# A hybrid layer on one core: attention scores head by head, with stacked queries and doubled keys

## The chip, the core and the metric

The kernel runs on one core of one Trainium2 chip. The core has five engines with an instruction queue each: TensorE (PE; its weight loads are shown apart as PEld), VectorE (DVE), ScalarE (ACT), GpSimd (POOL) and SyncE (SP), which here only issues DMAs. Operands lie in the on-chip memory SBUF, with 128 partitions; TensorE writes its products to PSUM, which this kernel uses as eight banks of 128 x 512 fp32.

The metric is the time of one execution in device microseconds. The kernel before takes 480.91 us, the median of three runs (480.37 to 481.25).

## What is computed

One layer for one sequence of 512 tokens of width 1024. Cut to its core:

```python
xn   = rmsnorm(h, norm_gain)
proj = xn @ w_in                  # split into aq ak av ag bq bf bi bg gate_a gate_b
qa, ka = rmsnorm(heads(aq)), rmsnorm(heads(ak))      # 8 heads x 64
ya = moba_attention(qa, ka, heads(av), rel_bias)     # softmax(q k^T / 8 + bias[bucket(distance)]) v
ya = (ya * silu(ag)) @ w_up_a
yb = hgrn2_chunkwise(silu(bq), kb(bf), bi, log_f(bf))  # gated linear recurrence, 4 heads x 128
yb = (rmsnorm(yb) * silu(bg)) @ w_up_b
merged = sigmoid(gate_a) * ya + sigmoid(gate_b) * yb
h = h + merged @ w_out
h = h + (p @ w_ple) * sigmoid(h @ w_ple_gate)
```

The sequence has two blocks of 256 keys and up to three blocks may be chosen, so every query attends to all keys up to its own position: the attention is causal and dense, with a bias by distance.

## The kernel before

**Numbers in two parts.** Large products are made in three: a value x is held as hi + lo, where hi is x rounded to the type fp32r (written by ScalarE) and lo the rest (written by VectorE), and hi·hi, hi·lo and lo·hi are summed in PSUM (`split`, `scale_split`, `mm3`, L189 to L253). A column block of weights (128 x 1024 values, 512 KB) is loaded by SP into one of two raw buffers `wf`, split into `wh` and `wl` (three buffers each), and used for 24 products of 512 columns. `weight` (L238) splits two blocks ahead (`LD = 2`).

**Main sequence.** TensorE goes through: the token-major projections bi and av, the first recurrence head's bf and bq, then aq and ak (queries and keys), then the list `ORDER` (L48) of feature-major blocks bg, ag, bf, gb, ga, then eight ub blocks (up-projection of the recurrence), eight ua blocks (of the attention), eight h blocks (output) and eight g and pe blocks (gated per-layer embedding).

**Side work and its order.** TensorE's order is the order in which the Python program issues it; the other engines are scheduled by the framework, with a priority raised by `AHEAD` for some. The program keeps a clock `now` in microseconds. Each product of the main sequence adds its cost (`tick`) and then lets generators whose due time has come issue their instructions (`run_due`, L107). A generator that yields y is due again y us later; `cost` adds time without looking at the generators. Generators run for the normalisation, the recurrence (`hgrn_intra`, `hgrn_out`), the preparation of queries and keys (`qk_norm`) and `attention`. `drain(name)` (L764) advances the clock in half microseconds, with no product of the main sequence, until the named part is done; ub waits in this way for the recurrence, ua for the attention.

**Queries and keys** (`qk_norm`, L635). The four token blocks of a projection are copied, squared, summed by head and scaled. 14 us later, for each of four head pairs, four 128 x 128 transposes put the pair's features on partitions (head 2i on partitions 0 to 63, head 2i+1 on 64 to 127), and `scale_split` makes hi and lo tiles: `qh`, `ql`, `kh`, `kl`, four of each, 16 tiles of pool `A`.

**Attention** (`attention`, L666). The queries are taken in `STEPS` (L31): blocks 0 and 1 of 128 queries together, then block 2, then block 3; block qb sees 128·(qb+1) keys. There are 12 steps, one for each head pair and entry of `STEPS`. In a step `scores` (L671) issues, for each query block, three products for each of the two heads; head j uses partitions 64j to 64j+63 of both operands, so that the two heads' products lie in two halves of the array (the profile writes 64*128), and they write to two banks of tag `a`. The softmax then takes, for each head and query block: VectorE adds the bias and finds the extreme (L689), ScalarE takes the exponential with its sum (L691), VectorE inverts the sum (L692) and scales (L693). One step later `transposed` (L697) transposes the probabilities of both heads, 128 x 128 at a time, and ScalarE copies them to SBUF (`ptS`). When the three steps of a pair are through, `out_values` (L711) multiplies by the values (o), VectorE gates the result (`ya`, L724), and `split` makes `yah` and `yal`, which the ua blocks read. A step is spread over `AP` = 12.2 us of the planner's clock: 0.3 of it before the transposes, 0.25 between them and the scores, 0.45 behind the scores. The bias of a head (128 x 512) is read by a DMA from a row in DRAM (`ed`), into a pool `T` of three.

**Recurrence.** `hgrn_intra` issues its products in two groups (lpb, lpa); ahead of each, while attention runs, `beside_attention` (L436) waits until attention has gone a step further or `BESIDE` = 5 us have passed.

Of the kernel before, what the change touches and what calls it, by code (L numbers as in the profile page):

```python
# [21 lines left out]
NT = S // 128  # L22
# [8 lines left out]
STEPS = ((0, 1), (2,), (3,))  # L31

HP = 3.1
AP = 12.2
H0 = 8.0
XN = 3.0

RT = 8.0

BESIDE = 5.0  # L40

LD = 2

# [15 lines left out]
def hybrid_layer_kernel(  # L59
# [24 lines left out]
    ctx.enter_context(tc.manual_schedule(engines=ENG))  # L84


    BUFS = {"w": 2, "wh": 3, "wl": 3, "A": 16, "X": 16, "YB": 8, "H": 12, "T": 3, "Q": 4, "KT": 2, "P": 4, "PT": 2,
            "PT0": 2, "PT2": 2, "SG": 4, "YS": 1, "VV": 8, "s32": 1, "st": 1, "ps": 8}

    def unit(tag, name, dt=F32, shape=(128, 512)):  # L90
        return sb.tile(list(shape), dt, tag=tag, bufs=BUFS[tag], name=name)

    def bank(tag, name):
        return psum.tile([128, 512], F32, tag=tag, bufs={"mm": 4, "g": 2, "a": 2}[tag], name=name)
# [98 lines left out]
    def scale_split(hi, lo, src, g):  # L193
        A.activation(hi, src, AF.Copy, scale=g)
        V.scalar_tensor_tensor(lo, src, g, hi.bitcast(F32), op0=OP.mult, op1=OP.subtract)
# [235 lines left out]

    hg = {}

    runs = [1000]

    def beside_attention():  # L436
        seen, until = runs[0], now[0] + BESIDE
        if seen < 1000:
            yield lambda: runs[0] > seen or now[0] >= until

    def hgrn_gates(h, F, Q):
        a = unit("H", f"ha{h}")
        A.activation(a, F, AF.Abs)
# [20 lines left out]
    def hgrn_intra(h):  # L464
# [52 lines left out]
        yield HP  # L517
        k16 = kq(16)
        yield HP
        yield from beside_attention()  # L520
        lpa = bank("g", f"lpa{h}").rearrange("p (l c t) -> p l c t", l=4, c=NT)
        for c in range(NT):
            o, i = c * 128, 64 * (c % 2)
# [20 lines left out]
        for b in (8, 4, 2):  # L544
            ks.append(kq(b))
            yield HP
        yield from beside_attention()
        for i, k_ in enumerate(ks):
            diag(lpa[:, 1 + i], k_, k_, LEVELS[1 + i])

# [82 lines left out]


    def qk_norm(name, banks, g, res):  # L635
        hs = [unit("A", f"{name}h{i}", R) for i in range(HPAIRS)]
        ls = [unit("A", f"{name}l{i}", R) for i in range(HPAIRS)]
        raws = []
        ss = cst.tile([128, NT, HEADS], F32, name=name + "ss")
        y = cst.tile([128, NT, HEADS], F32, name=name + "y")  # L640
        t_ = cst.tile([128, NT, HEADS], F32, name=name + "t")
        for t in range(NT):
            raw = unit("P", f"{name}r{t}")
            A.activation(raw, banks[t], AF.Copy)
            sq = unit("PT", f"{name}q{t}")
            A.activation(sq, raw, AF.Square)
            V.tensor_reduce(ss[:, t], sq.rearrange("p (h d) -> p h d", h=HEADS), axis=AX.X, op=OP.add)
            raws.append(raw)
        V.tensor_scalar(ss, ss, 1.0 / 64, None, op0=OP.mult)
        rsqrt(y, t_, ss)  # L650
        for t in range(NT):
            r3 = raws[t].rearrange("p (h d) -> p h d", h=HEADS)
            V.tensor_tensor(r3, r3, y[:, t, :, None].to_broadcast([128, HEADS, 64]), op=OP.mult)
        yield 14.0
        for i in range(HPAIRS):
            tp = bank("a", f"{name}tp{i}")
            for t in range(NT):
                PE.transpose(tp[:, t * 128:t * 128 + 128], raws[t][:, i * 128:i * 128 + 128], ident)
            cost(0.44)
            with tc.high_priority(offset=AHEAD):  # L660
                scale_split(hs[i], ls[i], tp, g)
            res.append((hs[i], ls[i]))
            yield 1.3
        done.add(name)

    def attention(qn, kn, va, sags, res):  # L666
        def blocks(qbs):

            return [(qb, sum(128 * (b + 1) for b in qbs[:i]), 128 * (qb + 1)) for i, qb in enumerate(qbs)]

        def scores(hp, qbs, T):  # L671
            (qh, ql), (kh, kl) = qn[hp], kn[hp]
            prs = []

            sps = [bank("a", f"s{hp}{qbs[0]}{j}") for j in range(2)]
            for qb, o, nk in blocks(qbs):
                qs = slice(qb * 128, qb * 128 + 128)
                for i, (a, b) in enumerate(((qh, kh), (ql, kh), (qh, kl))):
                    for j in range(2):
                        js = slice(64 * j, 64 * j + 64)  # L680
                        PE.matmul(sps[j][:, o:o + nk], a[js, qs], b[js, :nk], start=(i == 0), stop=(i == 2))  # L681
                cost(3 * max(0.107, nk * 0.00042))
            with tc.high_priority(offset=AHEAD):
                for j in range(2):
                    pr = unit("P", f"p{hp}{qbs[0]}{j}")
                    for qb, o, nk in blocks(qbs):
                        p_ = pr[:, o:o + nk]
                        st = unit("ps", f"ps{hp}{qb}{j}", shape=(128, 4))
                        V.tensor_tensor_reduce(p_, sps[j][:, o:o + nk], T[j][:, nk - 1::-1], -1.0, 3e38,  # L689
                                               OP.add, OP.min, st[:, 0:1])  # L690
                        A.activation(p_, p_, AF.Exp, bias=st[:, 0:1], scale=-1.0, accum_out=st[:, 1:2])  # L691
                        V.reciprocal(st[:, 2:3], st[:, 1:2])  # L692
                        V.tensor_scalar(p_, p_, st[:, 2:3], None, op0=OP.mult)  # L693
                    prs.append(pr)
            return prs

        def transposed(hp, qbs, prs):  # L697
            n = sum(qb + 1 for qb in qbs)
            pts = []
            for j in range(2):  # L700
                tp = bank("a", f"pt{hp}{qbs[0]}{j}")
                for kb in range(n):
                    PE.transpose(tp[:, kb * 128:kb * 128 + 128], prs[j][:, kb * 128:kb * 128 + 128], ident)  # L703
                cost(0.11 * n)
                pt = unit("PT" if n == NT else f"PT{qbs[0]}", f"ptS{hp}{qbs[0]}{j}", shape=(128, n * 128))
                with tc.high_priority(offset=AHEAD):
                    A.activation(pt, tp[:, :n * 128], AF.Copy)  # L707
                pts.append(pt)
            return pts

        def out_values(hp, pts):  # L711

            o = bank("mm", f"o{hp}")
            for qbs, pt in zip(STEPS, pts):
                for qb, o0, nk in blocks(qbs):
                    qs = slice(qb * 128, qb * 128 + 128)
                    for kb in range(qb + 1):
                        for j in range(2):
                            h0 = hp * 128 + 64 * j
                            PE.matmul(o[64 * j:64 * j + 64, qs], va[kb][:, h0:h0 + 64],  # L720
                                      pt[j][:, o0 + kb * 128:o0 + kb * 128 + 128], start=(kb == 0), stop=(kb == qb))
            cost(1.5)
            ya = unit("YS", f"ya{hp}")
            V.tensor_tensor(ya, o, sags[hp], op=OP.mult)  # L724
            h_ = unit("A", f"yah{hp}", R)
            l_ = unit("A", f"yal{hp}", R)
            split(h_, l_, ya)
            res.append((h_, l_))
            done.add(f"ya{hp}")

        while not {"q", "k"} <= done:
            yield lambda: {"q", "k"} <= done
        yield 3.0
        runs[0] = 0
        NS = len(STEPS)
        steps = [(hp, i) for hp in range(HPAIRS) for i in range(NS)]
        T, prs, pts = {}, {}, {}
        for n in range(len(steps) + 1):
            if n >= 2:
                yield AP * 0.3  # L740
            if 1 <= n <= len(steps):
                hp, i = steps[n - 1]
                pts[n - 1] = transposed(hp, STEPS[i], prs.pop(n - 1))
                yield AP * 0.25
            if n < len(steps):
                hp, i = steps[n]
                if i == 0:
                    for j in range(2):
                        t = unit("T", f"bias{hp}{j}")
                        row = ed[2 * hp + j:2 * hp + j + 1, :]  # L750
                        nc.sync.dma_start(t, bass.AP(tensor=row.tensor, offset=row.offset,
                                                     ap=[[1, 128], [1, 512]]))
                        T[hp, j] = t
                prs[n] = scores(hp, STEPS[i], [T[hp, 0], T[hp, 1]])
            if n >= 1 and steps[n - 1][1] == NS - 1:
                hp = steps[n - 1][0]
                while f"ag{hp}" not in done:
                    yield lambda: f"ag{hp}" in done
                out_values(hp, [pts.pop(n - NS + i) for i in range(NS)])
            runs[0] += 1  # L760
            yield AP * 0.45
        runs[0] += 1000

    def drain(name):  # L764

# [233 lines left out]
```

## Time and profile before

| what | before |
|---|---|
| median of three runs | 480.91 us |
| span of the profiled execution | 479.0 us |
| mean granted TensorE clock | 0.995 |
| first and last score product (start) | 140.1, 321.1 us |
| first and last transpose of probabilities | 149.4, 332.5 us |
| last product with values (start) | 338.3 us |
| first ub, first ua block | 329.7, 355.0 us |
| DMA traffic | 48.41 MB |

The profile shows one execution. Its table of engines gives busy time, share of the span and number of instructions. A row of a timeline gives the start, the duration, engine, line, operation, output and inputs, the shape (for a product: rows * columns of the array and the moving operand), how many are merged, and, in brackets, how long the engine was idle before it and what ended the idle time. Durations of products overlap their successors, so a product's price is the distance from start to start. A row of a list of waits names who waited for whom: total us, times, the longest. A row of the windows gives, behind the stretch and its length, the busy time of PE, PEld, DVE, ACT and POOL with the number of instructions, the granted TensorE clock, the DMA share and GB/s. A row of DMA issues gives tensors, queue, count, size and the median time to landing.

### The profile page before, as it was taken

How to read it: one execution, taken by the hardware profiler on the slowest of the kernel's cores; microseconds unless marked ns; L12 is line 12 of the kernel's file. 1: busy time of each engine (PE TensorE's matmuls, PEld its weight loads, DVE VectorE, ACT ScalarE, POOL GpSimd, SP SyncE). 2: the span in 40 equal slices, each digit the busy share in tenths (PEclk: the TensorE clock that was granted, in tenths of full speed). 3: DMA queues.
4: the chain of work that ended last, by engine and by line, in shares of the span. 5: the costliest groups of instructions: out<-in, count | busy, mean ns of one | idle time of the engine just before them, and what ended most of it. 6: DMA issues, size and time to landing. Idle time of an engine off the chain costs nothing.

```text
span 479.0 us, 7949 instructions
## 1 busy us (share of the span) xinstructions
PE 471.2 (98%) x3162; PEld 386.4 (81%) x3162; DVE 300.6 (63%) x601; ACT 269.4 (56%) x476; POOL 14.4 (3%) x30
## 2 busy tenths in 40 slices
PE   9999999999997999999999999999999999999996
PEld 7788888788875878878888788878888888888886
DVE  4769683957795784696757946435458854543332
ACT  5757665547695786687757766656324532243211
POOL 0014000000000001000010000000000000000000
PEclk9999999999998999999999999999999999999999
DMA  7542222332221222124212322124333544323211
GB/s 225 196 151 103 89 88 89 116 129 88 89 87 47 89 89 90 48 85 133 90 46 76 98 93 83 29 90 131 77 100 115 207 146 148 98 96 115 90 44 44
DMA packets 17941, 48.41 MB, mean 101 GB/s; under 512 B 2248, under 2 KB 2888, under 8 KB 17904
## 3 DMA queue, kind: packets, MB, share of 16 engines
q1 hardware_dynamic: 17616, 47.82, 30.8%
q8 instruction: 24, 0.39, 0.4%
q0 software_dynamic: 144, 0.09, 0.1%
q14 instruction: 13, 0.11, 0.1%
q10 hardware_dynamic: 144, 0.01, 0.0%
HBM read 45.79 MB, written 2.12 MB: 100 GB/s over the span
## 4 chain that ended last, share of the span: by engine, by line
PE 67%; ACT 1%; DVE 0%; issue 0%; DVEq 0%
PE gb L251 9%; PE g L251 9%; PE h L251 9%; PE ga L251 9%; PE ub L251 5%; PE ua L251 5%; PE ag L251 3%; PE bq L251 2%; PE bg L251 2%; PE bf L251 2%; PE pe L251 2%; PE o L720 2%; PE s L681 2%; PE pt L703 2%; PE lpa L501 1%; PE hds L581 0%
## 5 line engine op out<-in xcount | busy, mean ns | idle before, releaser
L190 ACT ACTIVATE wh<-wf 128x1024 fp32r<-128x1024 f32 (+1 forms) x81 | 77.6, 958 | 121.6 <-PE g L251 20.4
L191 DVE TENSOR_TENSOR wl<-wf,wh 128x1024 fp32r<-128x1024 f32 (+1 forms) x81 | 90.0, 1112 | 67.6 <-ACT wh L190 65.8
L251 PE MATMUL g<-hh,wh 128*128 128x512 f32 (+1 forms) x72 | 26.3, 365 | 0.0
L251 PE MATMUL g<-hl,wh 128*128 128x512 f32 (+1 forms) x72 | 26.3, 365 | 0.0
L251 PE MATMUL g<-hh,wl 128*128 128x512 f32 (+1 forms) x72 | 26.3, 365 | 0.0
L251 PE MATMUL ga<-xh,wh 128*128 128x512 f32 x64 | 26.0, 406 | 0.0
L251 PE MATMUL gb<-xh,wh 128*128 128x512 f32 x64 | 25.5, 398 | 0.0
L251 PE MATMUL ga<-xh,wl 128*128 128x512 f32 x64 | 25.0, 391 | 0.0
L251 PE MATMUL gb<-xh,wl 128*128 128x512 f32 x64 | 25.0, 390 | 0.0
L251 PE MATMUL gb<-xl,wh 128*128 128x512 f32 x64 | 25.0, 390 | 0.0
L251 PE MATMUL ga<-xl,wh 128*128 128x512 f32 x64 | 24.9, 390 | 0.0
L251 PE MATMUL h<-mh,wh 128*128 128x512 f32 x64 | 24.9, 389 | 0.0
L251 PE MATMUL h<-ml,wh 128*128 128x512 f32 x64 | 24.9, 389 | 0.0
L251 PE MATMUL h<-mh,wl 128*128 128x512 f32 x64 | 24.9, 389 | 0.0
L691 ACT ACTIVATE p<-p,ps 128x128 f32<-128x128 f32 (+3 forms) x32 | 17.6, 550 | 8.7 <-DVE ps L689 8.6
L689 DVE CUSTOM_DVE_ANT_0 p<-s,bias 128x128 f32<-128x128 f32 (+3 forms) x32 | 14.1, 486 | 7.5 <-PE s L681 7.5
L889 DVE TENSOR_TENSOR hf<-h,xres 128x512 f32<-128x512 f32 x8 | 5.5, 692 | 18.2 <-PE h L251 18.2
L707 ACT ACTIVATE ptS<-pt 128x384 f32<-128x384 f32 (+1 forms) x24 | 11.5, 524 | 7.5 <-PE pt L703 7.5
L251 PEld LDWEIGHTS g<-hh,wl 128*128 128x128 f32 x72 | 13.6, 189 | 2.2
L251 PEld LDWEIGHTS g<-hl,wh 128*128 128x128 f32 x72 | 13.6, 189 | 2.2
L480 ACT ACTIVATE hx<-hx 128x512 f32<-128x512 f32 x24 | 14.6, 627 | 1.2 <-DVE hx L479 0.9
L251 PEld LDWEIGHTS g<-hh,wh 128*128 128x128 f32 x72 | 13.6, 189 | 2.1
(326 smaller groups left out, 1245.8 us busy)
## 6 DMA issues: line engine op xcount, KB each, us to landing
wf<-in_w_tr_dram SPq DMA_DIRECT2D x32, 512.0 KB, 3.4
wf<-in_w_tok_dram SPq DMA_DIRECT2D x15, 512.0 KB, 3.4
wf<-in_w_up_dram SPq DMA_DIRECT2D x16, 256.0 KB, 2.6
wf<-in_w_o_dram SPq DMA_DIRECT2D x8, 512.0 KB, 3.3
wf<-in_w_g_dram SPq DMA_DIRECT2D x8, 512.0 KB, 3.5
bias<-ed SPq DMA_DIRECT2D x8, 256.0 KB, 3.4
xres<-in_xT_dram SPq DMA_DIRECT2D x8, 256.0 KB, 2.9
xr<-in_xT_dram SPq DMA_DIRECT2D x7, 256.0 KB, 5.8
```

Of the source, the lines that this page charges most:

```text
L190: A.activation(hi, src, AF.Copy)
L191: V.tensor_tensor(lo, src, hi.bitcast(F32), op=OP.subtract)
L251: PE.matmul(ps, a[:, k, :], b[k], start=(n == 0), stop=(n == tot - 1))
L480: A.activation(x, x, AF.Exp)
L501: PE.matmul(d, l[:, o:o + 32], m, start=True, stop=True)
L681: PE.matmul(sps[j][:, o:o + nk], a[js, qs], b[js, :nk], start=(i == 0), stop=(i == 2))
L689: V.tensor_tensor_reduce(p_, sps[j][:, o:o + nk], T[j][:, nk - 1::-1], -1.0, 3e38, OP.add, OP.min, st[:, 0:1])
L691: A.activation(p_, p_, AF.Exp, bias=st[:, 0:1], scale=-1.0, accum_out=st[:, 1:2])
L703: PE.transpose(tp[:, kb * 128:kb * 128 + 128], prs[j][:, kb * 128:kb * 128 + 128], ident)
L707: A.activation(pt, tp[:, :n * 128], AF.Copy)
L720: PE.matmul(o[64 * j:64 * j + 64, qs], va[kb][:, h0:h0 + 64], pt[j][:, o0 + kb * 128:o0 + kb * 128 + 128], start=(kb == 0), stop=(kb == qb))
L889: V.tensor_tensor(t, ps, xres, op=OP.add)
```

## The change

**Operands.** `qk_norm` ends in one of two new generators. `stacked_queries` makes one tile `qs` per head with 128 rows: the head's own 64 partitions hold hi, the other 64 hold lo of the same head (ScalarE writes the own half, VectorE the other). `doubled_keys` makes `kh` and `kl` for each head: the own half is written by ScalarE and VectorE, and two DMAs on SP's queue copy each half to the other 64 partitions, 16 DMAs of 128 KB in all. Queries and keys fill 24 tiles of pool `A` in place of 16; the pool grows from 16 to 24, and the DMA scratch in the compiler's call is set to 1024.

**Scores.** For each head and query block two products over all 128 rows are summed: [hi; lo] of the query with [kh; kh], then with [kl; kl]. This also adds lo·lo, which the kernel before left out.

**Order.** Attention goes through 24 steps (8 heads x 3) with `AP` = 6.1 in place of 12; the transposes of a step come `LAG` = 2 steps behind its scores in place of one; `out_values` comes at the start of the step behind the last transposes of a pair. The first two biases are loaded ahead of the steps, each further one two heads ahead. `beside_attention` goes; 2.5 us are yielded in its place, whether attention runs or not.

```diff
-AP = 12.2
+AP = 6.1
+LAG = 2
...
-BESIDE = 5.0
...
-    BUFS = {"w": 2, "wh": 3, "wl": 3, "A": 16, ...
+    BUFS = {"w": 2, "wh": 3, "wl": 3, "A": 24, ...
...
-        yield from beside_attention()
+        yield 2.5
...
+    def stacked_queries(raws, g, res):
+        for i in range(HPAIRS):
+            tp = bank("a", f"qtp{i}")
+            for t in range(NT):
+                PE.transpose(tp[:, t * 128:t * 128 + 128], raws[t][:, i * 128:i * 128 + 128], ident)
+            cost(0.44)
+            with tc.high_priority(offset=AHEAD):
+                for j in range(2):
+                    qs = unit("A", f"qs{2 * i + j}", R)
+                    own, other = slice(64 * j, 64 * j + 64), slice(64 - 64 * j, 128 - 64 * j)
+                    A.activation(qs[own], tp[own], AF.Copy, scale=g[own])
+                    V.scalar_tensor_tensor(qs[other], tp[own], g[own], qs[own].bitcast(F32),
+                                           op0=OP.mult, op1=OP.subtract)
+                    res.append(qs)
+            yield 1.5
+
+    def doubled_keys(raws, g, res):
...
+            for j in range(2):
+                kh = unit("A", f"kh{2 * i + j}", R)
+                kl = unit("A", f"kl{2 * i + j}", R)
+                own, other = slice(64 * j, 64 * j + 64), slice(64 - 64 * j, 128 - 64 * j)
+                with tc.high_priority(offset=AHEAD):
+                    scale_split(kh[own], kl[own], tp[own], g[own])
+                for k_ in (kh, kl):
+                    nc.sync.dma_start(k_[other].bitcast(F32), k_[own].bitcast(F32))
+                res.append((kh, kl))
+            yield 1.5
...
-                for i, (a, b) in enumerate(((qh, kh), (ql, kh), (qh, kl))):
-                    for j in range(2):
-                        js = slice(64 * j, 64 * j + 64)
-                        PE.matmul(sps[j][:, o:o + nk], a[js, qs], b[js, :nk], start=(i == 0), stop=(i == 2))
-                cost(3 * max(0.107, nk * 0.00042))
+                for i, k_ in enumerate(kn[h]):
+                    PE.matmul(sp[:, o:o + nk], qn[h][:, qs], k_[:, :nk], start=(i == 0), stop=(i == 1))
+                cost(2 * (nk + 32) / 2400)
...
-            cost(1.5)
+            cost(2.5)
...
+        T = {0: bias(0), 1: bias(1)}
         yield 3.0
...
+        steps = [(h, i) for h in range(HEADS) for i in range(NS)]
+        prs, pts = {}, {}
+        pending = None
+        for n in range(len(steps) + LAG + 1):
+            if pending is not None:
+                while f"ag{pending}" not in done:
+                    yield lambda: f"ag{pending}" in done
+                out_values(pending, pts)
+                pending = None
+            if LAG <= n < len(steps) + LAG:
+                h, i = steps[n - LAG]
+                pts[h, i] = transposed(h, STEPS[i], prs.pop(n - LAG))
+                if i == NS - 1 and h % 2:
+                    pending = h // 2
+                yield AP * 0.4
+            if n < len(steps):
+                h, i = steps[n]
+                prs[n] = scores(h, STEPS[i], T[h])
+                if i == 1 and h + 2 < HEADS:
+                    T[h + 2] = bias(h + 2)
+            yield AP * (0.6 if n >= LAG else 0.8)
...
-    nc = _bacc.Bacc("TRN2", target_bir_lowering=False, num_devices=1)
+    nc = _bacc.Bacc("TRN2", target_bir_lowering=False, num_devices=1,
+                    dynamic_dma_scratch_size=1024)
```

More of the change, by code (lines that the diff above doesn't have):

```diff
@@ L84, in hybrid_layer_kernel @@
     ctx.enter_context(tc.manual_schedule(engines=ENG))
-    BUFS = {"w": 2, "wh": 3, "wl": 3, "A": 16, "X": 16, "YB": 8, "H": 12, "T": 3, "Q": 4, "KT": 2, "P": 4, "PT": 2,
+    BUFS = {"w": 2, "wh": 3, "wl": 3, "A": 24, "X": 16, "YB": 8, "H": 12, "T": 3, "Q": 4, "KT": 2, "P": 4, "PT": 2,
             "PT0": 2, "PT2": 2, "SG": 4, "YS": 1, "VV": 8, "s32": 1, "st": 1, "ps": 8}
@@ L432, in hybrid_layer_kernel @@
     hg = {}
[L434 to L439, printed above, removed]
     def hgrn_gates(h, F, Q):
@@ L546, in hgrn_intra @@
             yield HP
-        yield from beside_attention()
+        yield 2.5
         for i, k_ in enumerate(ks):
@@ L635, in qk_norm @@
     def qk_norm(name, banks, g, res):
-        hs = [unit("A", f"{name}h{i}", R) for i in range(HPAIRS)]
-        ls = [unit("A", f"{name}l{i}", R) for i in range(HPAIRS)]
         raws = []
@@ L654, in qk_norm @@
         yield 14.0
+        if name == "q":
+            yield from stacked_queries(raws, g, res)
+        else:
+            yield from doubled_keys(raws, g, res)
+        done.add(name)
+    def stacked_queries(raws, g, res):
         for i in range(HPAIRS):
-            tp = bank("a", f"{name}tp{i}")
+            tp = bank("a", f"qtp{i}")
             for t in range(NT):
@@ L660, in qk_norm @@
             with tc.high_priority(offset=AHEAD):
[L661 to L664, printed above, removed]
+                for j in range(2):
[8 more added lines that the diff above has]
+        for i in range(HPAIRS):
+            tp = bank("a", f"ktp{i}")
+            for t in range(NT):
[11 more added lines that the diff above has]
+            yield 1.5
     def attention(qn, kn, va, sags, res):
@@ L669, in blocks, with scores @@
             return [(qb, sum(128 * (b + 1) for b in qbs[:i]), 128 * (qb + 1)) for i, qb in enumerate(qbs)]
[L671 to L675, printed above, removed]
+        def scores(h, qbs, T):
+            sp = bank("a", f"s{h}{qbs[0]}")
             for qb, o, nk in blocks(qbs):
                 qs = slice(qb * 128, qb * 128 + 128)
-                for i, (a, b) in enumerate(((qh, kh), (ql, kh), (qh, kl))):
-                    for j in range(2):
-                        js = slice(64 * j, 64 * j + 64)
-                        PE.matmul(sps[j][:, o:o + nk], a[js, qs], b[js, :nk], start=(i == 0), stop=(i == 2))
-                cost(3 * max(0.107, nk * 0.00042))
-            with tc.high_priority(offset=AHEAD):
[L684 to L695, printed above, removed]
@@ L697, in transposed @@
-        def transposed(hp, qbs, prs):
-            n = sum(qb + 1 for qb in qbs)
[L699 to L709, printed above, removed]
+                for i, k_ in enumerate(kn[h]):
+                    PE.matmul(sp[:, o:o + nk], qn[h][:, qs], k_[:, :nk], start=(i == 0), stop=(i == 1))
@@ new lines, in scores @@
+                cost(2 * (nk + 32) / 2400)
+            with tc.high_priority(offset=AHEAD):
+                pr = unit("P", f"p{h}{qbs[0]}")
+                for qb, o, nk in blocks(qbs):
+                    p_ = pr[:, o:o + nk]
+                    st = unit("ps", f"ps{h}{qb}", shape=(128, 4))
+                    V.tensor_tensor_reduce(p_, sp[:, o:o + nk], T[:, nk - 1::-1], -1.0, 3e38,
+                                           OP.add, OP.min, st[:, 0:1])
+                    A.activation(p_, p_, AF.Exp, bias=st[:, 0:1], scale=-1.0, accum_out=st[:, 1:2])
+                    V.reciprocal(st[:, 2:3], st[:, 1:2])
+                    V.tensor_scalar(p_, p_, st[:, 2:3], None, op0=OP.mult)
@@ new lines, in scores, with transposed @@
+            return pr
+        def transposed(h, qbs, pr):
+            n = sum(qb + 1 for qb in qbs)
+            tp = bank("a", f"pt{h}{qbs[0]}")
+            for kb in range(n):
+                PE.transpose(tp[:, kb * 128:kb * 128 + 128], pr[:, kb * 128:kb * 128 + 128], ident)
+            cost(0.11 * n)
+            pt = unit("PT" if n == NT else f"PT{qbs[0]}", f"ptS{h}{qbs[0]}", shape=(128, n * 128))
+            with tc.high_priority(offset=AHEAD):
+                A.activation(pt, tp[:, :n * 128], AF.Copy)
+            return pt
@@ L711, in out_values @@
         def out_values(hp, pts):
             o = bank("mm", f"o{hp}")
-            for qbs, pt in zip(STEPS, pts):
+            for i, qbs in enumerate(STEPS):
                 for qb, o0, nk in blocks(qbs):
@@ L720, in out_values @@
                             PE.matmul(o[64 * j:64 * j + 64, qs], va[kb][:, h0:h0 + 64],
-                                      pt[j][:, o0 + kb * 128:o0 + kb * 128 + 128], start=(kb == 0), stop=(kb == qb))
-            cost(1.5)
+                                      pts[2 * hp + j, i][:, o0 + kb * 128:o0 + kb * 128 + 128],
+                                      start=(kb == 0), stop=(kb == qb))
+            cost(2.5)
             ya = unit("YS", f"ya{hp}")
@@ L729, in out_values, with bias @@
             done.add(f"ya{hp}")
+        def bias(h):
+            t = unit("T", f"bias{h}")
+            row = ed[h:h + 1, :]
+            nc.sync.dma_start(t, bass.AP(tensor=row.tensor, offset=row.offset, ap=[[1, 128], [1, 512]]))
+            return t
         while not {"q", "k"} <= done:
             yield lambda: {"q", "k"} <= done
+        T = {0: bias(0), 1: bias(1)}
         yield 3.0
-        runs[0] = 0
         NS = len(STEPS)
-        steps = [(hp, i) for hp in range(HPAIRS) for i in range(NS)]
@@ L737, in attention @@
[L737 to L744, printed above, removed]
-            if n < len(steps):
[L746 to L761, printed above, removed]
@@ L762, in attention @@
-        runs[0] += 1000
+        steps = [(h, i) for h in range(HEADS) for i in range(NS)]
[13 more added lines that the diff above has]
+                yield AP * 0.4
+            if n < len(steps):
+                h, i = steps[n]
[3 more added lines that the diff above has]
+            yield AP * (0.6 if n >= LAG else 0.8)
```

## The prediction, made before the changed kernel ran

> **What bounds the kernel now.** I read the table of engines first, then what TensorE waits for.
>
> ```profile
> PE 471.2 (98%) x3162; PEld 386.4 (81%) x3162; DVE 300.6 (63%) x601; ACT 269.4 (56%) x476; POOL 14.4 (3%) x30
> ```
>
> ```profile
> PE pt L703 <- DVE p L693: 2.4, 2, 1.9
> ```
>
> TensorE is busy for 471.2 of 479.0 us, so the time is the length of TensorE's instruction stream, plus the few places where it stops. The only wait of weight in that list is 2.4 us, where the first transposes of probabilities wait for VectorE's scaling. Everything on the other engines is free as long as it does not make TensorE wait. The timeline of TensorE shows what the wait really costs:
>
> ```profile
> 147.06 0.39 PE L251 MATMUL ag<-xh,wl 128*128 128x512 f32 x1
> 149.37 0.90 PE L703 MATMUL pt<-ident,p 128*128 128x128 f32 x4 [1.92 <-DVE p L693]
> 150.75 0.69 PE L703 MATMUL pt<-ident,p 128*128 128x128 f32 x2 [0.48 <-DVE p L693]
> 151.09 0.78 PE L251 MATMUL ag<-xh,wh 128*128 128x512 f32 x1
> 151.66 0.63 PE L251 MATMUL ag<-xl,wh 128*128 128x512 f32 x1
> ...
> 153.37 0.40 PE L251 MATMUL ag<-xh,wl 128*128 128x512 f32 x1
> 153.61 0.40 PE L251 MATMUL ag<-xh,wh 128*128 128x512 f32 x1
> ```
>
> ```profile
> 150.00:160.00 10.00, 9.52 (x40) 7.23 (x39) 4.46 (x12) 5.08 (x10) 0.00 (x0) 0.83 0.34 104
> ```
>
> The projections start every 0.227 us elsewhere, and here, after the pause, every 0.43 us for five products; the granted clock of these ten microseconds is 0.83 (the column before the DMA share). To price it I need the undisturbed beats, from the chain of work that ended last:
>
> ```profile
> 168.75 0.66 PE pt L703 x6
> ...
> 355.12 21.76 PE ua L251 x96
> ...
> 468.72 5.76 PE g L251 x48
> ```
>
> 96 products of 512 columns take 21.76 us: 0.227 each. 48 products of 256 columns (the last output block, two halves) take 5.76: 0.120 each. Six transposes take 0.66: 0.11 each. From 147.06 to 153.61 are 6.55 us; they hold seven projection products (7 x 0.227 = 1.59) and six transposes (0.66). **The stall costs 6.55 - 2.25 = 4.3 us**, not 2.4.
>
> **The scores.** Three blocks, one of each kind of step, between two projection products:
>
> ```profile
> 139.82 0.39 PE L251 MATMUL bg<-xh,wl 128*128 128x512 f32 x1
> 140.14 0.33 PE L681 MATMUL s<-kh,qh 64*128 64x128 f32 x2
> ...
> 140.42 0.28 PE L681 MATMUL s<-kl,qh 64*128 64x128 f32 x2
> 140.53 0.33 PE L681 MATMUL s<-kh,qh 64*128 64x256 f32 x2
> 140.70 0.28 PE L681 MATMUL s<-kh,ql 64*128 64x256 f32 x2
> 140.82 0.28 PE L681 MATMUL s<-kl,qh 64*128 64x256 f32 x2
> 141.03 0.50 PE L251 MATMUL bg<-xh,wh 128*128 128x512 f32 x1
> 141.37 0.39 PE L251 MATMUL bg<-xl,wh 128*128 128x512 f32 x1
> 141.60 0.39 PE L251 MATMUL bg<-xh,wl 128*128 128x512 f32 x1
> ...
> 155.46 0.39 PE L251 MATMUL gb<-xh,wl 128*128 128x512 f32 x1
> ...
> 157.06 0.40 PE L251 MATMUL gb<-xh,wl 128*128 128x512 f32 x1
> ...
> 172.44 0.39 PE L251 MATMUL bq<-xh,wl 128*128 128x512 f32 x1
> ...
> 174.22 0.39 PE L251 MATMUL bq<-xh,wl 128*128 128x512 f32 x1
> ```
>
> Each block shares its stretch with three projection products (the one ahead and two behind; 3 x 0.227 = 0.68). So the blocks cost 1.78 - 0.68 = 1.10 us for queries 0 and 1 together, 1.60 - 0.68 = 0.92 for query block 2, and 1.78 - 0.68 = 1.10 for block 3: 3.12 per head pair, **12.5 us in four pairs**. The two heads of a pair do run at once: a pair of 128 columns follows the last by 0.11, one of 256 by 0.12, the price of one full product. With 0.11 + 0.12 + 0.173 + 0.227 (the third interpolated from the beats) times three, the pair would be 1.89 us; the other 1.23 are at the seams, where the first product of a block starts 0.32 after its predecessor and the projections behind it by 0.34: some 0.4 us for each of the three blocks.
>
> The change has two full-array products a head and query block. From the two beats a product of N columns takes 0.0133 + N x 0.000417 us: 0.227, 0.173, 0.120, and for 128 columns 0.067. The narrowest is not in the trace. Bounds: 0.067 by the line, and 0.11, at which both the transposes (full array, 128 columns) and the 128-column pairs run; I take 0.11, their row. A head is then 2 x 0.63 = 1.26 us, **eight heads 10.1 us** (9.4 with 0.067). At the seams I take nothing, since the full-array 256-column products run into 512-column ones and out again without a gap: 48 in 5.76 us leaves none. Upper bound: the 0.4 us of a tiled block, 24 times, 9.6 us. The gain is 12.5 - 10.1 = **2.4 us**; 3.1 with the lower price, a loss of 7.2 with the seams.
>
> [...]
>
> **Everything else that the change touches.**
>
> The transposes stay 80 at 0.11 us and the products with the values stay 160 records; only their grouping changes. Nothing on TensorE's account.
>
> The wait of 4.3 us: before, the planner puts the first transposes 0.45 x 12.2 = 5.5 us of TensorE work behind the scores (141.0 to 147.3 in the trace), and they were ready only at 149.4 and 150.8. After, two steps lie between: 2 x 0.8 x 6.1 = 9.8 us, plus their own 0.37 and 0.35, plus rounding up to the next tick of 0.68 twice: 10.5 to 11.9. Working all due times through, with the generators that interleave, I get 11.6. VectorE needed 8.3 us (141.0 to 149.4) for the first head and has one head to do in place of two. I take **-4.3**: the wait is gone. The later steps have the same distance, and waited nowhere even before.
>
> Query and key preparation: the queries' four ScalarE and four VectorE operations become eight each, at the same number of columns, and so do the keys'.
>
> ```profile
> 129.32 0.60 PE L658 MATMUL ktp<-ident,kr 128*128 128x128 f32 x4
> ```
>
> ```profile
> L194 ACT ACTIVATE kh<-ktp,sm x4: 686/689/693, 130.0 to 135.5; 128x512 fp32r<-128x512 f32 x4
> L195 DVE SCALAR_TENSOR_TENSOR kl<-ktp,sm,kh x4: 743/746/750, 130.7 to 136.6; 128x512 fp32r<-128x512 f32 x4
> ```
>
> That adds 4 x 0.69 = 2.8 us of ScalarE and 4 x 0.75 = 3.0 of VectorE, each for queries and for keys. Half as many partitions do not show in the trace; I take the same duration. TensorE covers it if the scores do not wait. By the due times the first key transposes move 2 us ahead (spacing, and lpa of the first head comes later), to about 127.2, and the first scores land at 140.8: 13.6 us apart. First key pair: transposes 0.44, ScalarE 0.69, VectorE 0.75, so the own halves stand at about 129.5.
>
> Then 16 DMAs of 128 KB on SP's queue double the keys.
>
> ```profile
> SPq L225 <- DVE wl L191: 305.4, 72, 13.3
> ```
>
> ```profile
> xr<-in_xT_dram SPq DMA_DIRECT2D x2, 128.0 KB, 3.5
> ```
>
> SP spends 305 us waiting to load weights, 305.4/72 = 4.2 each time, since a buffer is freed only by the low split. A key DMA may stand behind such a load: 129.5 + 4.2 + 3.5 = 137.2, ahead of 140.8 by 3.6 us. So no cost, with a cover that is not large. The other way, weight loads stand behind key DMAs that wait for ScalarE and VectorE for a microsecond or two; weights are split two blocks (10.9 us) ahead, which covers that. Bias loads: eight before and after; the first two go out before the scores either way.
>
> The end of attention: steps of 6.1 plus their own products come to 49.6 us a pair (36.6, 7.0 for products, 12 roundings of about 0.5), and LAG adds two steps. By the due times the last product with the values falls right behind the last ub block, where before it lay seven ub blocks ahead. So the chain to ya, which was hidden, lies before ua:
>
> ```profile
> 338.61 0.69 DVE L724 TENSOR_TENSOR ya<-o,ag3s 128x512 f32<-128x512 f32 x1 [1.08 <-PE o L720]
> ...
> 339.68 0.62 ACT L190 ACTIVATE yah<-ya 128x512 fp32r<-128x512 f32 x1
> ...
> 340.32 0.69 DVE L191 TENSOR_TENSOR yal<-ya,yah 128x512 fp32r<-128x512 f32 x1 [1.02 <-ACT yah L190]
> ```
>
> From the end of o the low part takes 341.0 - 338.5 = 2.5 us. The first ua block has nine products over the three older pairs (2.04 us) and one with yah before it needs yal: 2.27 us. I count **+0.3**; lower bound 0 (ScalarE's delay ahead of yah goes), upper 2.5.
>
> The shorter hgrn waits (2.5 us for up to 5), larger pool A and smaller DMA scratch cost TensorE nothing: factors and transposes of that branch are ready ahead of their place now, and stay so with 2 us less.
>
> **Sum:** -4.3 - 2.4 + 0.3 = -6.4 on a span of 479.0: 472.6. The median, 480.9, stands 1.9 above the span, so **474.5 us**.
>
> **Rivals.**
>
> A. The wait only moves. VectorE is nearly full just there:
>
> ```profile
> 120.00:132.00 12.00, 12.00 (x58) 9.97 (x57) 8.85 (x13) 7.56 (x11) 0.00 (x0) 1.00 0.26 88
> 132.00:140.00 8.00, 8.00 (x40) 6.36 (x39) 7.72 (x14) 7.08 (x13) 0.00 (x0) 1.00 0.19 66
> 140.00:150.00 10.00, 8.08 (x44) 6.22 (x43) 10.00 (x34) 8.45 (x21) 0.00 (x0) 1.00 0.16 55
> ```
>
> It (third of the busy columns) works 26.6 of these 30 us; 3.0 more for the keys and about 3.5 of the first hgrn head's normalisation, which comes 7 us later, overfill it by 3. The latency of 8.3 us then becomes 11.3 against a place 11.6 away. If it slips, the 4.3 us return in part or whole: up to 478.8. Against it: one head, not two, is scaled in that step. Chance 0.15, 476.5 to 479.9.
>
> B. Slower: the key DMAs come late. If the first stands behind the longest of SP's waits, 13.3 us, it lands at 129.5 + 13.3 + 3.5 = 146.3, 5.5 us after the scores' place; the slow clock raises that, as 2.4 became 4.3, to some 9.9: 474.5 + 9.9 = 484.4. It makes a loss once TensorE waits over 3.6 us (6.4 x 2.4 / 4.3). Against it: SP's waits average a third of that. Chance 0.07.
>
> C. The seams belong to any short block, not to the tiled mode. If each of 24 blocks pays 0.4, that is 9.6 more, 484.1 us; if every second does (12 x 0.4 = 4.9), the scores take 15.0, and the time is 479.0 - 4.3 + 2.5 + 0.3 + 1.9 = 479.4. From 0.27 us a block the whole gain is gone. The 256-column products without a gap and six transposes in 0.66 us speak against it. Chance 0.04 for each. [...]
>
> D. No measurable change (0.2%, 1.0 us, about what this measurement can tell): A whole with a quarter of C. Chance 0.06. Still better than forecast (0.067 us narrow products, and other small waits gone): below 472.5, chance 0.04.
>
> The forecast, 472.5 to 476.5, keeps 0.60. The range 472.0 to 480.0 takes in A and the milder C and leaves out B, the full C and D, 0.17. Faster: 0.60 + 0.15 + 0.04 + 0.04 = 0.83; same 0.06; slower 0.07 + 0.04 = 0.11.
>
> **What would show it.** Right: TensorE's list of waits has no pt behind VectorE's p, no stretch of clock 0.83 near 150, 24 score blocks with sums near 10 us and projections at 0.227 right behind them; the o block of the last pair directly ahead of ua. Wrong: s waiting for a DMA of kh or kl (B), projections 0.34 apart behind a score block (C), pt or ktp waiting for VectorE (A), ua waiting over 1 us for yah or yal.

## The result, and the profile after

The changed kernel takes 477.43 us, the median of six runs (477.11 to 478.82), against 480.83 for the kernel before in the same comparison. The ratio is 0.994 (95% interval 0.9924 to 0.9956). So it is faster, by 0.6 per cent. It lies inside the wide range of 472.0 to 480.0, but outside the forecast of 472.5 to 476.5 and in the band given to rival A: of 6.4 us that should have gone, 3.4 went.

First the table of engines of the changed kernel, then the list of what TensorE waited for, where a row gives total us, times and the longest:

```profile
PE 468.6 (99%) x3130; PEld 388.2 (82%) x3130; DVE 308.9 (65%) x609; ACT 274.2 (58%) x484; POOL 15.2 (3%) x30
```

```profile
PE ktp L673 <- DVE kl L194: 2.2, 2, 1.9
```

The wait of the first transposes of probabilities (pt behind p) is gone. A new one has the same size: the transposes of the keys (ktp) wait for VectorE's low halves. The timeline of TensorE shows it, with the idle time in brackets:

```profile
129.13 0.60 PE L673 MATMUL ktp<-ident,kr 128*128 128x128 f32 x4
...
131.42 0.40 PE L250 MATMUL bq<-xh,wl 128*128 128x512 f32 x1
132.11 0.63 PE L673 MATMUL ktp<-ident,kr 128*128 128x128 f32 x4 [0.29 <-DVE kl L194]
...
134.42 0.40 PE L250 MATMUL bq<-xh,wl 128*128 128x512 f32 x1
136.75 0.63 PE L673 MATMUL ktp<-ident,kr 128*128 128x128 f32 x4 [1.93 <-DVE kl L194]
```

A projection product takes 0.227, so the third transposes could have started at 131.65 and started at 132.11; the fourth could have at 134.65 and did at 136.75. TensorE loses 0.46 + 2.10 = **2.6 us**.

How long the attention stretch is, is read from the first aq and the first h product, on both sides of everything that the change touches; these rows of the operands' view give the first and the last start, of the kernel before and then of the changed one:

```profile
L411 PE MATMUL aq<-wh,xh x32: 389/389/389, 62.3 to 83.4; 128*128 128x512 f32 x32
L251 PE MATMUL h<-mh,wh x64: 389/389/389, 376.7 to 419.6; 128*128 128x512 f32 x64
```

```profile
L410 PE MATMUL aq<-wh,xh x32: 389/389/389, 61.5 to 82.6; 128*128 128x512 f32 x32
L250 PE MATMUL h<-mh,wh x64: 389/389/389, 373.3 to 416.1; 128*128 128x512 f32 x64
```

That is 314.4 us before and 311.8 after: **2.6 us** shorter. The profiled spans differ by 3.4 (479.0 and 475.6), but 0.8 of it lies ahead of aq, in work that both share. The experiments below start aq at 61.1 to 61.5 whichever kernel they are built on, so the 0.8 belongs to the one execution profiled of the kernel before. What a pause of TensorE costs also differs between executions of one program (spans of 475.6 and 477.0), which the last section takes up.

The scores came out as computed. The timeline of TensorE in the changed kernel, a block of query blocks 0 and 1, and one of block 2:

```profile
142.47 0.39 PE L250 MATMUL bg<-xh,wl 128*128 128x512 f32 x1
142.69 0.22 PE L696 MATMUL s<-kh,qs 128*128 128x128 f32 x1
142.75 0.28 PE L696 MATMUL s<-kl,qs 128*128 128x128 f32 x1
142.86 0.33 PE L696 MATMUL s<-kh,qs 128*128 128x256 f32 x1
...
143.15 0.40 PE L250 MATMUL bg<-xh,wh 128*128 128x512 f32 x1
143.39 0.39 PE L250 MATMUL bg<-xl,wh 128*128 128x512 f32 x1
...
148.37 0.39 PE L250 MATMUL ag<-xh,wl 128*128 128x512 f32 x1
148.60 0.33 PE L696 MATMUL s<-kh,qs 128*128 128x384 f32 x1
...
148.95 0.40 PE L250 MATMUL ag<-xh,wh 128*128 128x512 f32 x1
149.18 0.39 PE L250 MATMUL ag<-xl,wh 128*128 128x512 f32 x1
```

The first block starts 0.22 behind its predecessor and the projections go on at 0.24 and 0.23: there is no seam. It costs 0.92 - 0.45 = 0.47, the second 0.81 - 0.45 = 0.36. Over the 19 score blocks that stand alone among projections the mean is 0.43, so 24 make 10.3 us, against 12.5 before.

### The profile page after: what moved, and what is told of

It is laid out like the page before. It is cut to its first block, busy times and chain, and to the rows that moved or that the text cites. A ratio compares the mean times of both kernels' runs of the same rounds, so it can differ in the third digit from the quotient of the medians.

```text
span 475.6 us, 7956 instructions
## 1 busy us (share of the span) xinstructions
PE 468.6 (99%) x3130; PEld 388.2 (82%) x3130; DVE 308.9 (65%) x609; ACT 274.2 (58%) x484; POOL 15.2 (3%) x30
## 4 chain that ended last, share of the span: by engine, by line
PE 96%; DVE 1%; DMA 1%; SPq 0%; ACT 0%; issue 0%; DVEq 0%
PE gb L250 9%; PE ga L250 9%; PE g L250 9%; PE h L250 9%; PE ak L410 5%; PE ua L250 5%; PE bg L250 5%; PE bf L250 5%; PE ag L250 5%; PE ub L250 5%; PE av L410 5%; PE aq L410 5%; PE bq L250 4%; PE bi L410 4%; PE pe L250 2%; PE s L696 2%
## 5 line engine op out<-in xcount | busy, mean ns | idle before, releaser
L718 ACT ACTIVATE ptS<-pt 128x384 f32<-128x384 f32 (+1 forms) x24 | 12.5, 521 | 12.4 <-PE pt L714 12.1
```

## The experiments

Theory 1 is that the key transposes wait because a PSUM bank (they use the two of tag `a` in turn) stays occupied through a chain of four operations on two engines. Theory 2 is that VectorE simply has too much to do. All kernels below were timed beside the kernel before on one chip. e1 to e4 shared one set of runs of it (median 480.35), e5 to e7 another (479.88).

**e1: another order of the four operations, no work added or taken.**

```diff
-                with tc.high_priority(offset=AHEAD):
-                    scale_split(kh[own], kl[own], tp[own], g[own])
+            with tc.high_priority(offset=AHEAD):
+                for (kh, kl), (own, other) in zip(pair, halves):
+                    A.activation(kh[own], tp[own], AF.Copy, scale=g[own])
+                for (kh, kl), (own, other) in zip(pair, halves):
+                    V.scalar_tensor_tensor(kl[own], tp[own], g[own], kh[own].bitcast(F32),
+                                           op0=OP.mult, op1=OP.subtract)
```

> The changed kernel, with the four operations that read a key pair's PSUM bank in another order: both high halves on ScalarE, then both low halves on VectorE, in place of high, low, high, low. Theory 1 (the bank's chain): the last key transposes waited 2.1 us, and those before 0.5, because a bank is free only after four operations that hand over between the engines three times; with one handover the wait falls below 1 us, and the span from 475.6 to 473.5 to 474.5. Theory 2 (VectorE is simply full): the same operations take the same time in any order, the wait stays at 2 to 2.6 us and the span at 475.6.

Measured: 474.87 us (474.73 to 475.17), ratio 0.9889 (0.9872 to 0.9905), span 472.9. The wait is not smaller but gone, and the stretch from aq (61.3) to h (370.6) is 309.3 us, 2.5 less than in the changed kernel. Theory 2 has fallen: VectorE did the same work and was as full, 11.75 and 11.71 of the 12 us from 126 to 138 (the third busy column of the windows; the changed kernel, then e1):

```profile
126.00:138.00 12.00, 9.78 (x51) 7.63 (x50) 11.75 (x18) 9.65 (x16) 0.00 (x0) 1.00 0.57 165
```

```profile
126.00:138.00 12.00, 12.00 (x62) 9.96 (x61) 11.71 (x18) 10.78 (x17) 0.00 (x0) 1.00 0.72 202
```

What the chain looks like is seen on the timelines of ScalarE and VectorE. The changed kernel first, ScalarE:

```profile
127.42 0.67 ACT L193 ACTIVATE kh<-ktp,sm 64x512 fp32r<-64x512 f32 x1
129.82 0.68 ACT L193 ACTIVATE kh<-ktp,sm 64x512 fp32r<-64x512 f32 x1 [1.73 <-DVE kl L194]
...
132.01 0.68 ACT L193 ACTIVATE kh<-ktp,sm 64x512 fp32r<-64x512 f32 x1
...
135.00 0.68 ACT L193 ACTIVATE kh<-ktp,sm 64x512 fp32r<-64x512 f32 x1
```

and its VectorE:

```profile
129.05 0.74 DVE L194 SCALAR_TENSOR_TENSOR kl<-ktp,sm,kh 64x512 fp32r<-64x512 f32 x1
...
131.21 0.76 DVE L194 SCALAR_TENSOR_TENSOR kl<-ktp,sm,kh 64x512 fp32r<-64x512 f32 x1
...
133.28 0.74 DVE L194 SCALAR_TENSOR_TENSOR kl<-ktp,sm,kh 64x512 fp32r<-64x512 f32 x1
...
135.85 0.76 DVE L194 SCALAR_TENSOR_TENSOR kl<-ktp,sm,kh 64x512 fp32r<-64x512 f32 x1
```

then e1, ScalarE and VectorE:

```profile
127.20 1.38 ACT L679 ACTIVATE kh<-ktp,sm 64x512 fp32r<-64x512 f32 x2
129.54 1.39 ACT L679 ACTIVATE kh<-ktp,sm 64x512 fp32r<-64x512 f32 x2 [0.96 <-PE ktp L673]
```

```profile
128.83 1.53 DVE L681 SCALAR_TENSOR_TENSOR kl<-ktp,sm,kh 64x512 fp32r<-64x512 f32 x2
...
131.05 1.52 DVE L681 SCALAR_TENSOR_TENSOR kl<-ktp,sm,kh 64x512 fp32r<-64x512 f32 x2
```

In the changed kernel ScalarE stands idle for 1.73 us until the first low half has ended (129.05 + 0.74), though it reads other partitions and writes another tile: the compiled program makes the second high half wait for VectorE. That it does so because both read one PSUM tile is my reading; no run separates it. Each of the second pair's four then also queues behind other work of its engine and starts 0.02 to 0.03 us after that has ended, which is where the full engines come in. The second pair's bank is written from 129.13, and the last of its four operations ends at 136.6, 7.5 us later. In e1 the second pair is transposed at 128.9, and its last low half ends at 131.05 + 1.52 = 132.6, 3.7 us later.

**e2: more room between the key transposes.**

```diff
-            yield 1.5
+            yield 3.0
+            if i == 1:
+                done.add("k")
```

> The changed kernel with 3.0 us of planner time between the key transposes in place of 1.5; attention may start after the second pair, so that the scores keep their place. Theory 1: the banks are free when the third and fourth transposes come, no wait there, span 473.0 to 473.8 (2.6 less, if the scores find their bank free). Theory 2: VectorE is as full as before and the wait shows up at the first scores or the first transposes of probabilities; span 475 to 476.

Measured: 479.3 us (477.62 to 481.31), ratio 0.9989 (0.9973 to 1.0004), span 477.4, more than either theory gave. No transposes of keys wait any more, but the first scores do, 3.2 us. TensorE's timeline, and the low halves on VectorE's:

```profile
141.62 0.30 PE L698 MATMUL s<-kh,qs 128*128 128x128 f32 x1 [3.18 <-issue]
```

```profile
136.97 0.74 DVE L194 SCALAR_TENSOR_TENSOR kl<-ktp,sm,kh 64x512 fp32r<-64x512 f32 x1
140.76 1.53 DVE L194 SCALAR_TENSOR_TENSOR kl<-ktp,sm,kh 64x512 fp32r<-64x512 f32 x2
```

The view doesn't name the releaser. The scores need the bank of the third key pair, whose second low half is the first of the two merged from 140.76 and ended at about 141.5, 0.1 ahead of the scores. A wait at the first scores is what theory 2 expected, but theory 1 has it too once the next user of the tag meets a bank still held by the chain of four, so e2 doesn't decide between them; e1 does. My expectation overlooked that scores and key transposes share two banks. Behind this wait six projections start 0.43 us apart in place of 0.227, which adds some 1.2 us.

**e3: the kernel before, with only its wait taken away.**

```diff
+            if n == 1:
+                yield 5.0
             if 1 <= n <= len(steps):
```

> The kernel before with one edit: 5 us of planner time more ahead of the very first transposes of probabilities; nothing else of the change. It measures the wait term by itself. Theory 1: the wait of 2.4 us and the slow products behind it go together, 4.3 us, span 474.7, since attention ends seven ub blocks early and has room. Rival: only the idle 2.4 us go (476.6), or VectorE is late again at the next step (478 or more).

Measured: 475.35 us (475.11 to 476.91), ratio 0.9903 (0.9887 to 0.9919), span 473.6, no wait of pt. From aq (61.5) to h (371.3) are 309.8 us, 4.6 less than before; computed were 4.3. Some 0.4 of the 4.6 is another wait that went by the way: the second of two products of the recurrence (hms), which waited for VectorE in the kernel before and started 0.65 behind the first (318.74 to 319.39), here starts 0.24 behind it. These two lines alone gain more than the whole change (0.9903 against 0.994; for e7, the change again, 0.9955). Between e3 and e1, the two schemes of scores without their waits, lie 0.5 us on the same chip, and the intervals of their ratios overlap: that the new scores are worth anything beyond the small shift is not shown.

**e4: the changed kernel with one step of lag.**

```diff
-LAG = 2
+LAG = 1
```

> The changed kernel with LAG = 1: transposes one step behind their scores. Theory 1: the first come some 6 us behind the scores, VectorE needs over 8, so TensorE waits 2 us or more there, with slow products behind it: 2.5 to 4.5 us more than the changed kernel, 478 to 480. Rival: with one head in a step the softmax is through in 6 us, no wait returns and the second step of lag is worth nothing: 475 to 476.

Measured: 491.5 us (489.71 to 492.77), ratio 1.0228 (1.0204 to 1.0252), span 489.7. The direction was right and the size far too small: the waits come back in step after step, six of them in the list, and behind the first of them seven projections start 0.43 us apart.

```profile
PE pt L714 <- DVE p L707: 10.0, 6, 2.4
```

I had reckoned with the first step only. In the changed rhythm the transposes of any step come some 6 us behind its scores, and the softmax of one head, on two engines that serve the rest of the layer too, often takes longer: in the first step the scores started at 144.20 and VectorE released the transposes at 152.63, 8.4 us later. So at this spacing the change needs its second step of lag.

**e5 and e6: e1 with denser attention.**

```diff
-AP = 6.1
+AP = 5.5
```

> The kernel of e1 with AP = 5.5 in place of 6.1: attention runs denser, and by the due times the last product with the values comes behind the fourth ub block, no longer between the last ub and the first ua block. Theory (tail): the eight ua blocks took 22.3 us in place of 21.8 because they stood right behind it, so 0.4 to 0.6 us go; span 472.3 to 472.5, median 474.3. Rival: the softmax has 10 per cent less time from scores to transposes, and TensorE waits for VectorE somewhere; 474.9 or more.

> The kernel of e1 with AP = 5.8: by the due times the last product with the values still lands between ub and ua, so the tail stays. Theory (tail): as e1, 474.9 within 0.3. Rival (a denser attention is worth something by itself): half of what AP = 5.5 gives.

Measured: AP = 5.5 474.17 us, ratio 0.9888 (0.9873 to 0.9904); AP = 5.8 474.22, ratio 0.9889 (0.9873 to 0.9905). Against e1's 0.9889 neither can be told from no change. AP = 5.5 came out at the time expected, but not for the reason given, since AP = 5.8, whose tail stays, is as fast. On the chain of work that ended last, the end of AP = 5.5 reads

```profile
334.41 2.33 PE o L732 x40
348.57 21.76 PE ua L250 x96
```

and that of AP = 5.8

```profile
345.81 2.33 PE o L732 x40
348.14 22.27 PE ua L250 x96
```

So the 0.5 us in the ua blocks is real and goes when the last values come earlier, but AP = 5.5 reaches ua 0.4 later, and the sum is the same. Some 0.1 of these 0.4 is the seam behind the values: with AP = 5.8 the first ua product bears it (0.34 to the next one), with AP = 5.5 a ub product. The rest I didn't settle.

**e7: the changed kernel again**, as a base for these two.

> The changed kernel once more, on the chip of these runs, as the base for e5 and e6: 477.4 as before, 2.5 above e1.

Measured: 477.33 us (476.6 to 478.73), ratio 0.9955 (0.9938 to 0.9972). 3.1 us above e5 and e6, where 2.5 above e1 was expected. The best kernels of the study are e1, e5 and e6, 1.1 per cent faster than the kernel before.

## Where the prediction was right and where it failed

**The wait at the first transposes** (computed -4.3): right. It is gone in the changed kernel, and e3, which takes away nothing else by its edit, gained 4.6 between aq and h, of which some 0.4 lie at hms.

**The scores** (computed -2.4): right. 12.5 us became 10.3. Of the two products of 128 columns one follows after 0.06 and one after 0.11 us, so the value taken, 0.11 for each, was the upper of two true ones. The seams stood at the tiled score blocks (64*128 in the profile), with steps of 0.32 and 0.34; at the full-array blocks the steps are 0.22, 0.24 and 0.23, and rival C is out. What makes a seam no run shows. By the prediction's beats the paired products alone are 4 x 1.89 = 7.6 us, an estimate, which is less than the 10.3 of the full ones; it was the other 4.9 of the 12.5, at the seams, that made them dearer.

**The preparation of the keys** (computed as no cost): this is the step that failed. It said that TensorE covers the doubled work if the scores do not wait, and looked at the scores and the DMAs alone. The scores didn't wait and the DMAs landed in 2.2 (kh) and 2.3 us (kl) in the median (rival B is out). But the key transposes themselves go to two PSUM banks, and each bank is now held by four operations in strict alternation in place of two. The prediction added up the engines' busy time, 2.8 and 3.0 us, where it should have followed one bank from its transposes to its release: 7.5 us, with transposes coming every 2.5 us into two banks. It cost 2.6 us, which were put at nothing; e1 shows that the order of the four decides it. Rival A had the place right (ktp waiting for VectorE was named as one of its marks) and the time in its band, but partly by luck: it expected the transposes of probabilities to slip, and they did not wait. VectorE's load, its reason, lengthens each handover (the first four low halves start 0.17 to 0.96 us behind the end of their high halves, with VectorE at other work until then) but is not enough by itself, since e1 has the same load and no wait.

**Nothing for the regrouping:** wrong by some 0.8 us. The products with the values used to stand right behind a score block and now stand among projections. TensorE's timeline before, with the scores between the first two rows (left out) and one projection product ahead of the last row, and then after, again with one product left out:

```profile
236.94 0.39 PE L251 MATMUL gb<-xh,wl 128*128 128x512 f32 x1
...
238.14 2.40 PE L720 MATMUL o<-ptS,avv 128*64 128x128 f32 x40
...
240.81 0.39 PE L251 MATMUL gb<-xl,wh 128*128 128x512 f32 x1
```

```profile
201.83 0.39 PE L250 MATMUL gb<-xh,wl 128*128 128x512 f32 x1
202.15 2.40 PE L729 MATMUL o<-ptS,avv 128*64 128x128 f32 x40
204.49 0.55 PE L714 MATMUL pt<-ident,p 128*128 128x128 f32 x3
...
205.10 0.39 PE L250 MATMUL gb<-xl,wh 128*128 128x512 f32 x1
```

Before, scores and values together take 3.87 - 0.45 = 3.42, and without the 1.10 of a score block 2.32. After, values and three transposes take 3.27 - 0.45 = 2.82, and without the transposes' 0.35 (the mean of such blocks standing alone) 2.47. That is 0.15 more for three pairs, 0.45 us; the values of the last pair stood alone among projections before too, and cost 2.55 then and 2.54 now. I read it as a seam that the tiled scores had paid and that the values now pay themselves: they now start 0.32 behind a projection. The transposes in 24 groups at a mean of 0.38 make 9.1 us, against 80 x 0.11 = 8.8.

**The tail** (computed +0.3): 22.27 in place of 21.76, so 0.5. The mechanism was right: the first weight load with the last pair's low part waits for it. Some 0.1 of the 0.5 is the seam behind the values, which a ub product paid before.

```profile
351.14 22.27 PE ua L250 x96
```

```profile
353.63 0.19 PEld L250 LDWEIGHTS ua<-yal,wh 128*128 128x128 f32 x1 [0.39 <-DVE yal L190]
```

Together: -4.3 - 2.2 + 2.6 + 0.8 + 0.5 = -2.6, and -2.6 were measured between aq and h; that they meet to the tenth is luck. Without the key wait the sum would be -5.2, and e1 measured -5.1 (314.4 to 309.3). So of the 3.8 us between the forecast of -6.4 and the -2.6, the key wait is 2.6, and the regrouping most of the rest.

## What to carry to other kernels

A step that is said to be hidden has to be followed through each buffer that it holds, not only through the busy time of its engines: the question is when the bank comes free for the next write, and how many handovers between queues lie before that. Where two engines read one tile in turn, it can pay to let the first do all its parts before the second starts, as it did in e1. And before a scheme is replaced, try what a small shift of its own schedule gives: two lines in the old kernel were worth more than the new scheme as it stood.

## What the hardware showed unexpectedly

The same wait had two prices. In the profile of the changed kernel the products behind the 1.93 us of idle time run at the usual beat. In e7, the same program, they do not; TensorE's timeline, and a row of the windows with the granted clock (0.72) ahead of the last two numbers:

```profile
136.63 0.63 PE L673 MATMUL ktp<-ident,kr 128*128 128x128 f32 x4 [1.94 <-DVE kl L194]
...
137.33 0.54 PE L250 MATMUL bq<-xl,wh 128*128 128x512 f32 x1
137.67 0.63 PE L250 MATMUL bq<-xh,wl 128*128 128x512 f32 x1
...
140.23 0.63 PE L250 MATMUL bq<-xh,wl 128*128 128x512 f32 x1
140.66 0.48 PE L250 MATMUL bq<-xh,wh 128*128 128x512 f32 x1
140.97 0.40 PE L250 MATMUL bq<-xl,wh 128*128 128x512 f32 x1
```

```profile
138.00:143.00 5.00, 5.00 (x17) 3.95 (x17) 4.87 (x12) 3.21 (x6) 0.00 (x0) 0.72 0.69 159
```

For some 3.3 us a product takes 0.43 in place of 0.227, which adds about 1.5 us: the spans are 475.6 and 477.0. The six timed executions of the changed kernel fall into the same two groups, 475.3 to 475.7 us at a mean clock of 0.998 to 1.0, and 476.8 to 477.0 at 0.995; e1, with no wait, stays within 472.9 to 473.4. So in these runs a pause of 2 us was priced by chance between about 2 and 3.5 us. The kernel before has two prices too: of its 17 runs beside e1 to e4, five span 476.7 to 477.1 us at a clock of 0.998 to 0.999, and twelve 477.7 to 478.9 at 0.995 to 0.996. Its profile, with the 4.3 us, holds the higher price, and that of the changed kernel the lower; by e7's profile (61.4 to 374.7, 313.3 us) the stretch is only 1.1 us shorter than before, not 2.6.

What decides between the two prices no run shows. The slow products follow pauses of 1.94 us in e7 and of 3.18 in e2, while behind the 1.93 of the changed kernel there are none.
